# Recurrence stage of a bidirectional hybrid block: the inverse's products paired and moved, gate loads and chunk scalings re-placed

## The chip, the core and the metric

The kernel runs on one core of a Trainium2 chip. The metric is device time in microseconds (us) for one execution, the median of several. Five engines work side by side, each through its own queue in order: TensorE (PE in the profile; its weight loads are PEld), VectorE (DVE), ScalarE (ACT), GpSimd (POOL) and SyncE (SP), which here only issues DMAs. "The granted clock" (PEclk) is the share of TensorE's full speed that the chip allowed in a stretch.

## The reference

Cut to the part that the change touches; the other mixer, the projections and the MLP are left out.

```python
def _rwkv7_step(S, inp):
    """S_t = S_{t-1} diag(w_t) + (S_{t-1} a_t) b_t^T + v_t k_t^T ;  y_t = S_t r_t."""
    r, w, k, v, a, b = inp
    sa = jnp.einsum('bhvk,bhk->bhv', S, a)
    S = S * w[:, :, None, :] + sa[..., None] * b[:, :, None, :] + v[..., None] * k[:, :, None, :]
    y = jnp.einsum('bhvk,bhk->bhv', S, r)
    return S, y

# 8 heads of 64, 2048 tokens, once forward and once backward:
_, y_f = lax.scan(_rwkv7_step, S0, (r_s, ..., k_s, v_s, a_s, b_s))
_, y_b = lax.scan(_rwkv7_step, S0, (r_s, ..., k_s, v_s, a_s, b_s), reverse=True)
y = y_f + y_b                      # then a group norm per head, a bonus term, a gate g
...
merged = jax.nn.sigmoid(gate_a) * y_a + jax.nn.sigmoid(gate_b) * y_b
x = x + merged @ w_out
```

## The kernel before, in words

The kernel is one program of many stages. The change touches the recurrence stage. There the 2048 tokens are cut into 32 chunks of 64, and a loop runs over the steps s = 0 to 31; step s handles chunk s of the forward scan and chunk 31 - s of the backward one, for all 8 heads at once.

Within a step the recurrence is a chain: `st_W` (products of the chunk with the state X, evicted by ACT into W), `st_U` (W times the inverse TT, evicted by ACT into X), `st_S` (the state's increment; DVE adds it to gX and writes the next X, L1022; gX is then made by L999) and `st_Y` (the output, evicted by ACT). `sc_mm` computes the scores of a chunk LA = 7 steps ahead, for d = 0 and d = 1 apart; `sc_ev` evicts them: two DVE multiplies with a mask (Q, psc: L880, L881) and ACT copies (Nb, Lt: L887, L889). `tr_mm`/`tr_ev` transpose the operand bj of the next step, and `scale_bj` scales it by a decay: four ACT instructions for each d (L902).

The inverse TT is made for four chunks in both directions together, by the generator `invert`: DVE transposes the scores (XX, L919), runs 30 elimination steps (L924, L925), and transposes the result back in two halves into one buffer XC (L932). ACT copies each half into TT, four copies a half (L938); since XC is a single buffer, the second half waits for the first half's copies. DVE then makes the transposed result XT (L940), and TensorE forms the corner block in two products, first pz = Q times XT, then px = zs times TT, each for two halves hf = 0 and 1. The generator is cut by `yield`s: each plain `yield` gives up a VEC slot (`bg` takes one), each `yield "pe"` waits for a PE slot (`sl.tick(PE)`). It is started at the end of each fourth step and its TT is needed by the `st_U` of the fourth step after.

TensorE's free time is filled by `fill`, a generator of 312 slots of four 128x512 matmuls each: first 36 gate units (kind "g", six slots), then 32 output units (kind "y", three slots). The loop draws two slots at each of four places in a step (FW, F2, F3, F4), the part ahead of the loop draws others, and what is left follows the loop. Each change of weights brings a 512 KB load, an ACT cast (whi) and a DVE subtraction (wlo). A y unit loads its gate (`g_get`, into one of the three buffers `ev`), has ACT take the sigmoid in place (`g_sig`), and DVE multiplies it with the unit's PSUM result (L1221); the product goes out by DMA from the same buffer. In the last steps `gn_out` normalises the finished chunks, with some multiplies on POOL.

What sets the order: inside the loop PE, ACT, DVE and POOL work in the order in which the code is written (`manual_schedule`), each engine strictly one instruction after the other. The order of SP's loads is chosen by the framework's scheduler. Tags and `bufs` set which buffer a tile reuses, and so which instruction waits for which.

Of the kernel before, what the change touches and what calls it, by code (L numbers as in the profile page):

```python
# [166 lines left out]
def _body(tc, A, out, dump=None, upto=99):  # L167
# [749 lines left out]
    def invert(n):  # L917
# [22 lines left out]
        nc.vector.transpose(xt.rearrange("p b c -> p c b"), X)  # L940
        yield
        yield "pe"
        for hf in range(2):
            pz = cq.tile([128, 16, 32], F32, name="pz", tag="ptr")
            for u in range(16):
                sd, p = hf * 4 + u // 4, u % 4
                Q = qs[(n * 4 + sd // 2, sd % 2)][1]
                for e in range(2):
                    a0 = e * 64
                    nc.tensor.matmul(pz[a0 + 32:a0 + 64, u, :], Q[a0:a0 + 32, p, 32:64], xt[a0:a0 + 32, sd * 4 + p, :], start=True, stop=True)  # L950
            zs = cp.tile([128, 16, 32], F32, name="zs", tag="XX", bufs=2)
            nc.scalar.copy(out=zs[32:64], in_=pz[32:64])
            nc.scalar.copy(out=zs[96:128], in_=pz[96:128])
            yield "pe"
            px = cq.tile([128, 16, 32], F32, name="px", tag="ptr")
            for u in range(16):
                sd, p = hf * 4 + u // 4, u % 4
                for e in range(2):
                    a0 = e * 64
                    nc.tensor.matmul(px[a0:a0 + 32, u, :], zs[a0 + 32:a0 + 64, u, :], tt[a0 + 32:a0 + 64, sd, p, 32:64], start=True, stop=True)  # L960
            for e in range(2):
                a0 = e * 64
                (nc.scalar.copy if e else nc.vector.tensor_copy)(
                    out=tt[a0:a0 + 32, hf * 4:hf * 4 + 4, :, 32:64], in_=px[a0:a0 + 32].rearrange("r (a b) c -> r a b c", a=4))
            yield "pe"

# [67 lines left out]
    def gn_out(i):  # L1034
# [37 lines left out]
        for t in range(2):  # L1072
            nc.gpsimd.tensor_tensor(out=y8[t], in0=y8[t], in1=b8(rr[:, t * 8:t * 8 + 8]), op=ALU.mult)  # L1073
        yield
# [12 lines left out]
        for t, tt in enumerate(tiles):  # L1087
            nc.vector.tensor_tensor(out=o[t], in0=o[t], in1=bon[t], op=ALU.add)
            nc.gpsimd.tensor_tensor(out=o[t], in0=o[t], in1=gg[t], op=ALU.mult)
            sync.dma_start(out=d_ob[:, :, tt * 128:tt * 128 + 128], in_=o[t])  # L1090
# [31 lines left out]
    def fill():  # L1122
# [71 lines left out]
        for u, (kind, m, b) in enumerate(units):  # L1194
            if kind == "y":
                at(first[u] - 1, g_get, u)
                at(first[u] + 1, g_sig, u)

# [56 lines left out]
    bjs = [load_bj(1, d) for d in range(2)]  # L1255
    for d in range(2):
        scale_bj(1, d, bjs[d])
    for y in inv0:
# [12 lines left out]

    GN0, GNC, GNS = 27, [0], 3

# [5 lines left out]
    with tc.manual_schedule(engines=ORDERED):  # L1279
        for s in range(32):  # L1280
            la = s + LA
            last = s == 31
            st_W(s)
            bg(2)
            sl.tick(PE)
# [11 lines left out]
            if la < 32:  # L1297
                c = sc_mm(la, 0)
                sc_ev(c)
            bg(2)  # L1300
            sl.tick(PE)
# [3 lines left out]
            if not last:  # L1305
# [5 lines left out]
                st_g(s + 1)  # L1311
            st_Y(s)
            if la < 32:
                c = sc_mm(la, 1)
                sc_ev(c)
            if s % 4 == 0 and s < 28:
                sl.add(invert(s // 4 + 1))
            bg(2)
            sl.tick(PE)
            gn_tick(s, 1)  # L1320
            fil(F3)
            for d in range(2):
                if s < 30:
                    scale_bj(s + 2, d, bjs[d])
                bg(2)
                gn_tick(s, 2)
            sl.tick(PE)
            fil(F4)
    while gns or go.gens:
        gn_tick(32, 1)  # L1330
        fil()
    fil(1000)
# [486 lines left out]
```

## Time and profile before

| what | value |
|---|---|
| median of 3 runs | 3625.32 us (3624.73 to 3634.07) |
| profiled execution, its own time | 3635.12 us |
| its span in the profile | 3633.3 us |
| recurrence stage within the span, first slot of `fill` to the last transposes of `gn_out` | about 1052 to 1963 us |
| PE busy over the whole span | 3291.2 us (91%) |
| DVE / ACT / POOL busy | 2319.6 / 1569.8 / 1003.0 us |

The rows are read like this. A timeline row gives the start, the length, the engine, the line of the program, the operation and its operands, and in brackets how long the engine had been idle just before and whose end released it. A row of waits sums such idle times for one pair of instruction and releaser: total us, how often, the longest. Idle time matters on the engine that sets the pace; here that question has to be asked stretch by stretch.

### The profile page before, as it was taken

The numbers are of one execution on the slowest core, as the hardware profiler recorded it, in microseconds if no ns is written. First come the engines' busy times: TensorE is split into PE (matmuls) and PEld (weight loads), VectorE is DVE, ScalarE is ACT, GpSimd is POOL, SyncE is SP. The second block draws the span as 40 slices with busy tenths as digits, with TensorE's granted clock in tenths as the row PEclk, the third lists the DMA queues.
The fourth block names the chain that finished last, engine by engine and source line by source line (L and its number), as shares of the span: only waits on it lengthen the run. The fifth ranks groups of instructions, "written<-read, shape, count | busy, mean of one in ns | idle before, by whom it ended". The sixth has DMA issues, their size and how long they took to land. (4 is left out here: it accounts for less than half of the span.)

```text
span 3633.3 us, 58213 instructions
## 1 busy us (share of the span) xinstructions
PE 3291.2 (91%) x22232; PEld 2622.3 (72%) x22232; DVE 2319.6 (64%) x3913; ACT 1569.8 (43%) x2870; POOL 1003.0 (28%) x789
## 2 busy tenths in 40 slices
PE   7999999998978878877767899999989999999999
PEld 6787778766657666666655788877768777778887
DVE  5207764688846665666766466989899989724222
ACT  4214443555546666666544333434344443511111
POOL 1122222244430000000024412676766666100000
PEclk9999999999988999998988999999989999999999
DMA  4233444688883545555788746322232222523222
GB/s 148 91 118 109 134 137 134 197 224 229 230 247 108 158 151 158 153 182 177 216 244 271 286 140 199 115 76 79 78 125 96 81 76 82 168 86 115 83 83 64
DMA packets 403223, 531.30 MB, mean 146 GB/s; under 512 B 61504, under 2 KB 250560, under 8 KB 402944
## 3 DMA queue, kind: packets, MB, share of 16 engines
q1 hardware_dynamic: 402944, 527.58, 46.5%
q8 instruction: 175, 2.87, 0.3%
q14 instruction: 104, 0.85, 0.1%
HBM read 345.02 MB, written 181.93 MB: 145 GB/s over the span
## 5 line engine op out<-in xcount | busy, mean ns | idle before, releaser
L1553 POOL TENSOR_TENSOR rw<-rw 128x512 f32<-128x512 f32 x168 | 274.4, 1653 | 4.6 <-DVE cv L1598 1.2
L1706 PE MATMUL pd<-wdh,whi 128*128 128x512 f32 x672 | 261.6, 391 | 1.6 <-DVE ug L1498 1.6
L1707 PE MATMUL pd<-wdl,whi 128*128 128x512 f32 x672 | 261.4, 389 | 0.0
L1708 PE MATMUL pd<-wdh,wlo 128*128 128x512 f32 x672 | 259.3, 389 | 0.0
L241 PE MATMUL pg<-hhi,whi 128*128 128x512 f32 x928 | 249.0, 403 | 3.1 <-ACT whi L226 3.1
L241 PE MATMUL pg<-hlo,whi 128*128 128x512 f32 x928 | 250.5, 402 | 0.0
L241 PE MATMUL pg<-hhi,wlo 128*128 128x512 f32 x928 | 248.7, 403 | 0.0
L1073 POOL TENSOR_TENSOR Lt<-Lt,rnr 128x512 f32<-128x512 f32 x16 | 19.4, 1234 | 824.9 <-DVE rnr L254 766.5
L241 PEld LDWEIGHTS pg<-hhi,whi 128*128 128x128 f32 x928 | 176.2, 192 | 54.4 <-issue 14.3
L241 PEld LDWEIGHTS pg<-hhi,wlo 128*128 128x128 f32 x928 | 176.1, 192 | 49.8 <-issue 13.6
L241 PEld LDWEIGHTS pg<-hlo,whi 128*128 128x128 f32 x928 | 174.0, 191 | 52.4 <-issue 17.5
L227 POOL TENSOR_TENSOR wlo<-wraw,whi 128x1024 fp32r<-128x1024 f32 x46 | 114.9, 2498 | 349.6 <-PE pg L241 157.8
L1213 PE MATMUL pf<-fop,whi 128*128 128x512 f32 x576 | 172.6, 438 | 39.1 <-ACT whi L226 23.6
L1597 ACT ACTIVATE cv<-ug,vec 128x511 f32<-128x511 f32 (+1 forms) x88 | 71.9, 817 | 249.5 <-DVE ug L1498 249.5
L226 ACT CAST whi<-wraw 128x1024 fp32r<-128x1024 f32 x114 | 119.3, 1046 | 114.3 <-PE pg L241 50.8
L1213 PEld LDWEIGHTS pf<-fop,whi 128*128 128x128 f32 x576 | 113.7, 207 | 71.6 <-ACT whi L226 28.5
L1695 ACT CAST whi<-wraw 128x1024 fp32r<-128x1024 f32 (+1 forms) x36 | 35.2, 979 | 265.9 <-PE pd L1707 180.5
L1706 PEld LDWEIGHTS pd<-wdh,whi 128*128 128x128 f32 x672 | 126.1, 188 | 30.7 <-issue 5.0
L1598 DVE SCALAR_TENSOR_TENSOR cv<-ug,vec,cv 128x511 f32<-128x511 f32 (+1 forms) x88 | 125.0, 1421 | 35.8 <-ACT cv L1597 35.8
L227 DVE TENSOR_TENSOR wlo<-wraw,whi 128x1024 fp32r<-128x1024 f32 x68 | 83.7, 1231 | 99.4 <-ACT whi L226 98.8
L1708 PEld LDWEIGHTS pd<-wdh,wlo 128*128 128x128 f32 x672 | 126.2, 188 | 26.2
L1707 PEld LDWEIGHTS pd<-wdl,whi 128*128 128x128 f32 x672 | 126.2, 188 | 25.6
(470 smaller groups left out, 8274.4 us busy)
## 6 DMA issues: line engine op xcount, KB each, us to landing
rw<-wup SPq DMA_DIRECT2D x84, 512.0 KB, 3.5
wraw<-win SPq DMA_DIRECT2D x74, 512.0 KB, 4.1
Lt<-d_lt SPq DMA_DIRECT2D x64, 512.0 KB, 5.6
d_lt<-arbk SPq DMA_DIRECT2D x96, 256.0 KB, 3.9
d_gate<-ev SPq DMA_DIRECT2D x64, 256.0 KB, 3.5
X<-d_vt SPq DMA_DIRECT2D x64, 256.0 KB, 4.6
bj<-d_lt SPq DMA_DIRECT2D x128, 128.0 KB, 3.9
d_m<-ev SPq DMA_DIRECT2D x64, 256.0 KB, 5.4
```

The source lines that it names most:

```text
L226: (hi_eng or nc.scalar.copy)(out=hi, in_=src)
L227: (lo_eng or nc.vector).tensor_tensor(out=lo, in0=src, in1=hi.bitcast(F32), op=ALU.subtract)
L241: nc.tensor.matmul(ps, (wh, wh, wl)[ph], (xh, xl, xh)[ph], start=(ph == 0 and i == 0), stop=(ph == 2 and i == n - 1))
L1073: nc.gpsimd.tensor_tensor(out=y8[t], in0=y8[t], in1=b8(rr[:, t * 8:t * 8 + 8]), op=ALU.mult)
L1213: nc.tensor.matmul(ps, (wh, wh, wl)[ph][:, k0 + k, :], (hi, lo, hi)[ph][:, k, :], start=i == first[u] and k == 0, stop=i == last[u] and k ...
L1553: ps_ = lambda o, x, y, op: nc.gpsimd.tensor_tensor(out=o, in0=x, in1=y, op=op)
L1597: nc.scalar.activation(out=c, in_=u[:, c0:c0 + n], func=AF.Identity, scale=vc("cw1", m), bias=vc("cb", m))
L1598: nc.vector.scalar_tensor_tensor(out=c, in0=u[:, c0 - 1:c0 - 1 + n], scalar=vc("cw0", m), in1=c, op0=ALU.mult, op1=ALU.add)
L1695: nc.scalar.copy(out=ah[:, 0:n], in_=raw[:, 0:n])
L1706: nc.tensor.matmul(ps, a, wdh[k][:, cs], start=(k == 0), stop=False)
L1707: nc.tensor.matmul(ps, a, wdl[k][:, cs], start=False, stop=False)
L1708: nc.tensor.matmul(ps, l, wdh[k][:, cs], start=False, stop=False)
```

## The change

- `invert`: three more empty VEC slots between XT and the first product; pz of both halves in one PE slot, px of both halves in one PE slot, with a PE slot left empty between them. Half 1 takes its PSUM from the tag `psc` instead of `ptr`. The copies of px: both of half 0 on DVE, both of half 1 on ACT.
- The VEC slots of a step (`bg`): 14 before; now 12, and 14 in the fresh steps that start an inversion, of which 7 lie behind the start where 6 did.
- `g_get` is written two slots earlier, at the unit's first slot minus 3; `g_sig` one slot later, at its last slot.
- `scale_bj`: both directions were scaled behind F3; now d = 1 is scaled behind the W eviction and d = 0 behind the Y eviction.
- `gn_out`: both POOL multiplies go to DVE; the first `gn_out` starts at step 26 instead of 27; the loop behind the steps draws two fill slots a round instead of one.

```diff
@@ invert
         nc.vector.transpose(xt.rearrange("p b c -> p c b"), X)
         yield
+        for _ in range(3):
+            yield
         yield "pe"
+        zz = []
         for hf in range(2):
-            pz = cq.tile([128, 16, 32], F32, name="pz", tag="ptr")
+            pz = (cf.tile if hf else cq.tile)([128, 16, 32], F32, name="pz", tag="psc" if hf else "ptr", bufs=3 if hf else 1)
...
             nc.scalar.copy(out=zs[96:128], in_=pz[96:128])
-            yield "pe"
-            px = cq.tile([128, 16, 32], F32, name="px", tag="ptr")
+            zz.append(zs)
+        yield "pe"
+        yield "pe"
+        for hf in range(2):
+            px = (cf.tile if hf else cq.tile)([128, 16, 32], F32, name="px", tag="psc" if hf else "ptr", bufs=3 if hf else 1)
...
-                (nc.scalar.copy if e else nc.vector.tensor_copy)(
+                (nc.scalar.copy if hf else nc.vector.tensor_copy)(
                     out=tt[a0:a0 + 32, hf * 4:hf * 4 + 4, :, 32:64], in_=px[a0:a0 + 32].rearrange("r (a b) c -> r a b c", a=4))
-            yield "pe"
@@ gn_out
-            nc.gpsimd.tensor_tensor(out=y8[t], in0=y8[t], in1=b8(rr[:, t * 8:t * 8 + 8]), op=ALU.mult)
+            nc.vector.tensor_tensor(out=y8[t], in0=y8[t], in1=b8(rr[:, t * 8:t * 8 + 8]), op=ALU.mult)
...
-            nc.gpsimd.tensor_tensor(out=o[t], in0=o[t], in1=gg[t], op=ALU.mult)
+            nc.vector.tensor_tensor(out=o[t], in0=o[t], in1=gg[t], op=ALU.mult)
@@ fill
-                at(first[u] - 1, g_get, u)
-                at(first[u] + 1, g_sig, u)
+                at(first[u] - 3, g_get, u)
+                at(last[u], g_sig, u)
@@ ahead of the loop
-    for d in range(2):
-        scale_bj(1, d, bjs[d])
+    scale_bj(1, 0, bjs[0])
@@ the loop over the steps
-    GN0, GNC, GNS = 27, [0], 3
+    GN0, GNC, GNS = 26, [0], 3
...
             st_W(s)
+            if not last:
+                scale_bj(s + 1, 1, bjs[1])
             bg(2)
...
-            bg(2)
+            bg(1)
             sl.tick(PE)
             gn_tick(s, 1)
             fil(F2)
...
             st_Y(s)
+            if s < 30:
+                scale_bj(s + 2, 0, bjs[0])
...
-            bg(2)
+            bg(3 if fresh else 2)
             sl.tick(PE)
             gn_tick(s, 1)
             fil(F3)
-            for d in range(2):
-                if s < 30:
-                    scale_bj(s + 2, d, bjs[d])
-                bg(2)
-                gn_tick(s, 2)
+            bg(2)
+            gn_tick(s, 2)
+            bg(2 if fresh else 1)
+            gn_tick(s, 2)
             sl.tick(PE)
             fil(F4)
     while gns or go.gens:
         gn_tick(32, 1)
-        fil()
+        fil(2)
```

Three places show what this does to the order; all are the second inversion that the loop makes (started behind step 4, needed by step 8). On PE before, from the last scores of step 6 to the state products of step 7 (psc are scores, pf fill slots, pw and py the products of `st_W`):

```order
L874 MATMUL psc<-Lt 64x128 x16
L1213 MATMUL pf<-hhi_110,wlo 128x512 x4
L1213 MATMUL pf<-fop,whi 128x512 x4
L950 MATMUL pz<-XT,Q 32x32 x32
L1213 MATMUL pf<-fop,whi 128x512 x4
L1213 MATMUL pf<-fop,wlo 128x512 x4
L985 MATMUL pw<-X,Lt 64x64 x16
L992 MATMUL py<-X,Lt 64x64 x16
L960 MATMUL px<-TT_8672,zs 32x32 x32
```

On PE now, from the same scores on (ptr is the transpose of bj, pu the products of `st_U`):

```order
L874 MATMUL psc<-Lt 64x128 x16
L1218 MATMUL pf<-fop,whi 128x512 x8
L1218 MATMUL pf<-fop,wlo 128x512 x4
L1218 MATMUL pf<-fop,whi 128x512 x4
L990 MATMUL pw<-X,Lt 64x64 x16
L997 MATMUL py<-X,Lt 64x64 x16
L1218 MATMUL pf<-fop,whi 128x512 x4
L1218 MATMUL pf<-fop,wlo 128x512 x4
L908 MATMUL ptr<-ident,bj 128x128 x4
L1014 MATMUL pu<-W,TT_8673 64x64 x16
L874 MATMUL psc<-Lt 64x128 x16
L953 MATMUL pz<-XT,Q 32x32 x64
```

The first product stood between F3 and F4 of step 6; now it stands behind the first scores of step 7, with both halves together.

On DVE before, the end of the same inversion around the state update of step 6 (X, gX):

```order
L924 TENSOR_TENSOR tm<-XX 128x30
L925 TENSOR_TENSOR XX<-XX,tm 128x30
L928 MEMSET XX 128x32
L932 STREAM_TRANSPOSE XC<-XX 128x16x32
L1022 TENSOR_TENSOR X<-pS,gX 64x8x64 x2
L999 TENSOR_TENSOR gX<-X,gall 64x512 x2
L880 TENSOR_TENSOR Q<-psc,mk_8666 128x512
L881 TENSOR_TENSOR psc<-psc,mk_8666 128x512
L932 STREAM_TRANSPOSE XC<-XX 128x16x32
L940 STREAM_TRANSPOSE XT<-XX 128x32x32
```

On DVE now:

```order
L1027 TENSOR_TENSOR X<-pS,gX 64x8x64 x2
L1004 TENSOR_TENSOR gX<-X,gall 64x512 x2
L880 TENSOR_TENSOR Q<-psc,mk_8670 128x512
L881 TENSOR_TENSOR psc<-psc,mk_8670 128x512
L924 TENSOR_TENSOR tm<-XX 128x58
L925 TENSOR_TENSOR XX<-XX,tm 128x2x29
L924 TENSOR_TENSOR tm<-XX 128x30
L925 TENSOR_TENSOR XX<-XX,tm 128x30
L928 MEMSET XX 128x32
L932 STREAM_TRANSPOSE XC<-XX 128x16x32
L227 TENSOR_TENSOR fop<-ev,fop 128x512 x2
L932 STREAM_TRANSPOSE XC<-XX 128x16x32
```

The last two elimination steps and the first half of XC stood ahead of the state update and now stand behind it; XT follows directly, as before.

On ACT before, from the evictions of step 6's last scores to the W of step 7:

```order
L889 COPY Lt<-psc 64x512 x2
L938 COPY TT_8672<-XC 32x32x16 x4
L1217 COPY ev<-pf 128x512
L902 ACTIVATE bj<-bj,gall 128x128 x4
L938 COPY TT_8672<-XC 32x32x16 x4
L902 ACTIVATE bj<-bj,gall 128x128 x4
L952 COPY zs<-pz 32x512
L953 COPY zs<-pz 32x512
L226 CAST whi<-wraw 128x1024
L226 CAST fop<-ev 128x512 x2
L987 COPY W<-pw 128x512
```

On ACT now, from the same evictions on:

```order
L889 COPY Lt<-psc 64x512 x2
L226 CAST fop<-ev 128x512 x2
L938 COPY TT_8672<-XC 32x32x16 x6
L992 COPY W<-pw 128x512
L902 ACTIVATE bj<-bj,gall 128x128 x4
L938 COPY TT_8672<-XC 32x32x16 x2
L1222 COPY ev<-pf 128x512
L913 COPY bkt<-ptr 128x512
```

The scalings no longer stand ahead of W, and two of the four copies of the second half of XC now follow it; six copies, two of them from the second half, stand ahead of it.

## Rows read from the trace of the kernel before

**Rows 1.** Busy time by stretch: from:to, length, busy by engine, PEclk, DMA, GB/s.

```profile
1172.30:1734.00 561.70, 444.41 (x7900) 365.99 (x7896) 344.57 (x658) 368.08 (x803) 0.00 (x0) 0.91 0.53 164
1734.00:1908.00 174.00, 120.39 (x1605) 97.51 (x1600) 117.99 (x232) 87.56 (x182) 21.62 (x16) 0.85 0.78 232
1908.00:1963.00 55.00, 32.33 (x110) 24.14 (x109) 42.10 (x96) 26.96 (x59) 23.12 (x16) 0.72 0.79 253
```

**Rows 2.** PE's waits from 1040 to 1945 us: total us, times, longest.

```profile
PE pz L950 <- DVE XT L940: 73.1, 8, 14.2
PE pf L1213 <- ACT whi L226: 45.9, 18, 11.2
PE pu L1009 <- ACT W L987: 16.8, 10, 6.1
```

**Rows 3.** PE timeline, steps 4 to 7: start, us, instruction, [idle before, releaser].

```profile
1247.24 1.15 PE L985 MATMUL pw<-X,Lt 128*64 128x64 f32 x32
...
1251.74 1.09 PE L1009 MATMUL pu<-W,TT 64*64 64x64 f32 x30
...
1259.21 0.96 PE L1213 MATMUL pf<-hlo,whi 128*128 128x512 f32 x3
...
1263.06 1.15 PE L985 MATMUL pw<-X,Lt 128*64 128x64 f32 x32
...
1277.99 1.20 PE L1213 MATMUL pf<-hhi,whi 128*128 128x512 f32 x4 [2.04 <-ACT whi L226]
...
1314.14 1.92 PE L950 MATMUL pz<-XT,Q 32*32 32x32 f32 x64 [14.18 <-DVE XT L940]
1315.98 2.08 PE L1213 MATMUL pf<-fop,whi 128*128 128x512 f32 x4
...
1321.32 1.20 PE L960 MATMUL px<-TT,zs 32*32 32x32 f32 x64
```

**Rows 4.** DVE timeline: first, second and seventh inversion of the loop.

```profile
1172.31 2.17 DVE L919 STREAM_TRANSPOSE XX<-Nb 128x1024 f32<-128x1024 f32 x1 [0.68 <-ACT Nb L887]
...
1262.21 2.15 DVE L919 STREAM_TRANSPOSE XX<-Nb 128x1024 f32<-128x1024 f32 x1 [0.68 <-ACT Nb L887]
...
1300.67 0.21 DVE L924 TENSOR_TENSOR tm<-XX 128x58 f32<-128x58 f32 x1
...
1302.64 1.36 DVE L1022 TENSOR_TENSOR X<-pS,gX 64x512 f32<-64x512 f32 x2
...
1311.12 1.09 DVE L932 STREAM_TRANSPOSE XC<-XX 128x512 f32<-128x512 f32 x1 [4.37 <-ACT TT L938]
...
1733.94 2.07 DVE L919 STREAM_TRANSPOSE XX<-Nb 128x1024 f32<-128x1024 f32 x1 [0.68 <-ACT Nb L887]
```

**Rows 5.** ACT timeline, the end of the second inversion.

```profile
1306.18 1.22 ACT L887 COPY Nb<-Q 32x128 f32<-32x128 f32 x4 [5.76 <-DVE Q L880]
1307.41 1.17 ACT L889 COPY Lt<-psc 64x512 f32<-64x512 f32 x2
1308.60 2.49 ACT L938 COPY TT<-XC 32x512 f32<-32x512 f32 x4
...
1320.51 0.59 ACT L987 COPY W<-pw 128x512 f32<-128x512 f32 x1 [0.54 <-PE pw L985]
```

**Rows 6.** PE timeline at the start of the loop, step 0.

```profile
1147.48 1.92 PE L960 MATMUL px<-TT,zs 32*32 32x32 f32 x64 [3.85 <-ACT zs L953]
...
1158.38 1.86 PE L1009 MATMUL pu<-W,TT 64*64 64x64 f32 x29
```

**Rows 7.** Waits of ACT and of SP's queue for the gates, 1040 to 1945 us.

```profile
ACT ev L1192 <- DMA ev<-d_gate: 51.3, 13, 9.9
...
SPq L1189 <- DMA d_m<-ev: 70.8, 24, 8.2
```

**Rows 8.** The end of the stage: a PE timeline row, and POOL's multiply by line.

```profile
1917.45 2.11 PE L1081 MATMUL psc<-ident,Lt 128*128 128x128 f32 x8 [9.11 <-POOL Lt L1073]
...
L1073 POOL TENSOR_TENSOR Lt<-Lt,rnr 128x512 f32<-128x512 f32 x12 | 14.0, 1186 | 824.9 <-DVE rnr L254 766.5 <-DMA Lt<-d_y 27.9 <-DMA Lt<-d_bon 16.0
```

More of the change, by code (lines that the diff above doesn't have):

```diff
@@ L959, in invert @@
                     a0 = e * 64
-                    nc.tensor.matmul(px[a0:a0 + 32, u, :], zs[a0 + 32:a0 + 64, u, :], tt[a0 + 32:a0 + 64, sd, p, 32:64], start=True, stop=True)
+                    nc.tensor.matmul(px[a0:a0 + 32, u, :], zz[hf][a0 + 32:a0 + 64, u, :], tt[a0 + 32:a0 + 64, sd, p, 32:64], start=True, stop=True)
             for e in range(2):
                 a0 = e * 64
-                (nc.scalar.copy if e else nc.vector.tensor_copy)(
+                (nc.scalar.copy if hf else nc.vector.tensor_copy)(
                     out=tt[a0:a0 + 32, hf * 4:hf * 4 + 4, :, 32:64], in_=px[a0:a0 + 32].rearrange("r (a b) c -> r a b c", a=4))
-            yield "pe"
     def load_x(s):
@@ L1282, in _body @@
             last = s == 31
+            fresh = s % 4 == 0 and s < 28
             st_W(s)
+            if not last:
+                scale_bj(s + 1, 1, bjs[1])
             bg(2)
@@ L1315, in _body @@
                 sc_ev(c)
-            if s % 4 == 0 and s < 28:
+            if fresh:
                 sl.add(invert(s // 4 + 1))
-            bg(2)
+            bg(3 if fresh else 2)
             sl.tick(PE)
```

## The prediction, made before the changed kernel ran

> **What bounds the kernel now.** I read the busy times by stretch first. The diff touches only the recurrence stage, so the stretches around it keep their times. Within the stage no engine is full: from the first inversion of the loop to the seventh, 561.7 us, PE is busy for 444.4, ACT for 368.1 and DVE for 344.6 us, and the granted clock averages 0.91 [rows 1]. Such shares hide what limits each part, so I went to PE's waits. The largest is the first product pz, waiting for DVE's transpose XT: 73.1 us in 8 waits, one for each inversion; behind it come fill slots that wait for ACT's cast whi, 45.9 us in 18, and `st_U` waiting for W, 16.8 us in 10 [rows 2].
>
> The PE timeline says how much there is to win. An undisturbed step runs from 1247.24 to 1263.06, 15.8 us [rows 3]. A period of four steps with four products of some 1.2 us would so need 4 x 15.8 + 4.8 = 68.1 us. The six periods between the first and the seventh inversion of the loop take (1733.94 - 1172.31) / 6 = 93.6 us each [rows 4]: 25.5 us of each are waiting and slow clock.
>
> In the second inversion DVE starts at 1262.21, when PE has just passed the second scores of step 4, and writes the state X of step 6 at 1302.64 + 1.36 = 1304.00, 41.8 us later [rows 4]. The order of DVE puts every state update behind the elimination steps written ahead of it. PE stands idle for 14.18 us until 1314.14, waiting for XT [rows 3]. So the path of this part runs through DVE and, at its end, to and fro between DVE and ACT: ACT idles 5.76 us for Q, copies Nb and Lt, then the first half of XC into TT for 2.49 us, and DVE waits 4.37 us for those copies before the second half [rows 4, 5].
>
> **The change part by part.** The new place of the products does not shorten DVE's work by one instruction. It puts more of PE's work ahead of the wait: F4 of step 6 (1.9 us), and of step 7 all up to the first scores. I add up a period of the second inversion along what ends last.
>
> (a) From the start of the inversion to X of step 6: 41.8 us before. The last two elimination steps and the first half of XC, from 1300.67 to 1302.64, 2.0 us, now stand behind this update [rows 4]: 39.8 us.
>
> (b) From X to W of step 7. W is now behind six TT copies on ACT, and two of these need the second half of XC. From X at 1304.00 to the end of Q at 1306.18 2.2 us; Nb and Lt 2.4; four copies 2.5; the half of XC 1.1; two copies half of 2.5, 1.25; the W copy 0.6 [rows 4, 5]: 10.05, and 0.75 for an ACT instruction of a fill slot that stands between: 10.8 us. XT on DVE is done by then, so pz itself waits no more; the wait moves to the state products and to `st_U`.
>
> (c) From `st_U` of step 7 to the next inversion: a step without its first 4.5 us (1247.24 to 1251.74), 11.3 us; four products, 4.8; from step 8's start to the inversion as from 1247.24 to 1262.21, 15.0 [rows 3, 4]: 31.1. After the long wait pz took 1.92 against 1.20 and a fill slot 2.08 against 1.20 us [rows 3], which fits the lower level of the clock, 1.2 against 2.4 GHz. I estimate 2.2 us for this a period, before and after, since a wait of some 6 us for W remains; and 1.0 us for the transposition that waits for the buffer `ptr` behind the zs copies, now four in a row. 34.3 us.
>
> Together 39.8 + 10.8 + 34.3 = 84.9. The same sum on the kernel before, 41.8 + 10.1 to pz + 1.9 + 15.8 + 4.8 + 15.0 + 2.2 + 1.1 = 92.7, falls 0.9 short of 93.6, small waits for whi; added, 85.8. That is 7.8 us an inversion, and I take 8, for seven inversions **56 us**. Bounds: 4 an inversion if X is no earlier and the copies around W cost 2 us more; 13 if the divided wait leaves the clock up, `ptr` is free and DVE waits 2 us less for ACT (the scalings, no longer ahead of whi and W, let ACT reach whi earlier; a wait of 2.04 us left the clock up [rows 3]). So 28 to 91.
>
> The order of ACT is what keeps (b) long. ACT stood idle 5.76 us at Nb with copies written behind it [rows 5]; it passes nothing. The Trainium skill ("TensorE: Matmul & The Clock Gate", the architectural detail on queue depths) calls the queues of ScalarE and VectorE strictly first in, first out. If ACT could take W ahead of the copies, `st_U` would start some 6 us sooner, and pz would be held only by XT, about 2 us a period less: seven times that would make the sum 14 us better; by the rule and the row it is not.
>
> **The first products, ahead of step 0.** There px waited 3.85 us for zs, and the halves followed one another, product and copies in turn, until `st_U` at 1158.38, 10.9 us behind the first px [rows 6]. With both halves at once one round of copies goes. The order also puts four more fill slots (4.1 us) there, which now cover the copies and are missing at the end of the stage. I take **5 us**, between 2 (copies on ACT as late as before) and 8.
>
> **The gates.** Written earlier is not loaded earlier. A gate lands in one of three buffers `ev`, which the previous output of two units before, or a load of the fill's operand, leaves only when its DMA has landed: SP already waits for d_m 24 times, 70.8 us [rows 7], 2.95 us each. Moving the load up two slots leaves that bound where it is. What is real is the sigmoid, one slot later: a slot is 15.8 / 8 = 2.0 us, and ACT's 13 waits for gates, 51.3 us, 9.9 the longest [rows 7], shrink by up to 2.0 each, at most 26 us. About half of it holds W or a transposition that PE needs. **10 us**, between 0 and 25.
>
> **The rest.** The transposes of `gn_out` cost PE one wait of 9.11 us for POOL; POOL's multiply took 1.19 us [rows 8], where DVE's adds took 0.68 each [rows 4]. 32 of them are some 22 us of DVE in the last 170 us of the stage, in which DVE has 69 us idle (174.0 - 118.0 and 55.0 - 42.1) [rows 1]: covered, but each stands ahead of a fill product in DVE's order. One step's head start for `gn_out` takes seven of its slots out of the last 55 us, of which PE is busy 32 [rows 1]. The four slots moved to the front cost this end nothing while it waits. **6 us**, between -4 (multiplies in DVE's way) and 15.
>
> Sum: 56 + 5 + 10 + 6 = 77 us. The profiled execution took 3635.1 us outside, 3633.3 in its span, 10 over the median of 3625.3; I take the gain off both: 3558 for such an execution, **3548** for the median. With all lower bounds (28 + 2 + 0 - 4 = 26) 3599, with all upper ones (91 + 8 + 25 + 15 = 139) 3486.
>
> **The rivals.**
> - The stall only moves. If X of step 6 is as late as before, and W follows it by 9 us more than in (b), the 8.9 us of PE work set ahead of pz are eaten. For: DVE does the same work, and ACT's chain through XC now stands in front of W. Against: the longest part of (b) was in the path before too. It leaves the start and a little of the gates: 3617.
> - DVE stops being the bound. If the scalings behind the evictions let ACT keep up, and DVE with it, a period nears PE's own 68.1 + 4 = 72 us: 21 x 7 + 21 = 168 off, 3457. Against: (a) is mostly DVE's own work, and none of it is taken away.
> - The gates do come early, as the words of the change say: then ACT's 51.3 us go, and of PE's losses some 35 instead of 10: 3523. Against: the ring of three buffers.
> - Slower: the gate's early load blocks SP. It is now issued behind d_m at once and holds the loads of bj, X and weights behind it until d_m has landed. Before, 24 holds of 2.95 us. If each doubled and PE saw all of it, 24 x 5.9 = 142 us would be lost, 3690; from 77 / 24 = 3.2 us a unit on the change is slower than before. Against: SP's order is chosen apart from the engines', and already puts most loads behind such a wait.
>
> The Trainium skill ("DMA: Bandwidth & Descriptors", Anatomy of one DMA) says that DMA engines don't wait on semaphores, the issuing sequencer does, before it dispatches. That speaks against writing a load ahead of its free buffer, and for the last rival; SP's 70.8 us [rows 7] agree that the wait is SP's.
>
> **How the numbers follow.** A change of 0.3%, 11 us, is about what a measurement of this kernel can tell from none. Forecast 0.65; early gates 0.13; DVE no bound 0.08; the stall only moves 0.07, which counts as the same; slower 0.07. Faster so has 0.86. The range takes the forecast with its bounds and the early gates, 0.78, and a little of the faster side: 3490 to 3600.
>
> **What would show it.** Right: periods between inversions of 84 to 87 us; pz with hardly a wait; new waits of `st_W` for X and of `st_U` for W, some 6 to 9 us together an inversion, the latter behind ACT's TT copies; SP's waits at the gate about as long as before. Wrong: periods below 80, then DVE's lag was not the path; pz still waiting 5 us or more, then XT is later than (b) says; `st_S` or the transposition waiting for X or bj loads in steps 21 to 31, then the gates block SP.

## The result, and the profile after

| kernel | median | ratio to before, 95% interval |
|---|---|---|
| before | 3627.57 us (4 runs) | 1 |
| after | 3572.49 us (3569.51 to 3574.50, 4 runs) | 0.9845 [0.9828, 0.9862] |

The changed kernel is 1.55% faster, some 56 us. The forecast was 77 us and 3548; the time lies inside the range of 3490 to 3600. Below, the gain of a kernel is always (1 - ratio) x 3630 us, 3630 being about the median of before over all comparisons; intervals of 0.0009 to 0.0019 to either side mean that such a gain is known to 3 to 7 us, and the difference of two of them mostly to 8 or 9.

The profiled span fell from 3633.3 to 3568.9 us. That is 9 us more than the medians are apart, since the profiled execution of before was a long one (3635.12 us against a median of 3627.57); a stretch read from one execution of each carries such differences. By stretch, from after's own inversions: busy times and clock (from:to, length, busy by engine, PEclk, DMA, GB/s), to set beside [rows 1]:

```profile
1166.88:1690.91 524.03, 440.37 (x7873) 363.48 (x7872) 345.42 (x660) 369.35 (x803) 0.00 (x0) 0.93 0.58 177
1690.91:1842.60 151.69, 109.18 (x1494) 88.74 (x1494) 115.72 (x240) 81.44 (x170) 0.00 (x0) 0.85 0.87 249
1842.60:1997.40 154.80, 124.97 (x614) 98.46 (x613) 96.67 (x168) 69.66 (x117) 55.44 (x37) 0.90 0.90 313
```

The first line is the stretch from the first to the seventh inversion of the loop, 561.7 us before [rows 1]. PE's idle time in it fell from 117.3 us (561.7 - 444.4) to 83.7, its busy time only by 4.0: the gain is waiting taken away. The second line is the seventh inversion to the start of step 31 (161.0 before), the third from there to the first product with `w_out` (164.4 before); the merge of the two mixers, whose products begin some 51 us behind the start of step 31 in both kernels, lies within it.

The inversions themselves, DVE timeline of after (start, us, instruction, [idle before, releaser]): the first, second, third, sixth and seventh, and the second state update within the second one.

```profile
1166.88 2.05 DVE L919 STREAM_TRANSPOSE XX<-Nb 128x1024 f32<-128x1024 f32 x1 [0.68 <-ACT Nb L887]
...
1250.93 2.07 DVE L919 STREAM_TRANSPOSE XX<-Nb 128x1024 f32<-128x1024 f32 x1 [0.68 <-ACT Nb L887]
...
1290.03 1.38 DVE L1027 TENSOR_TENSOR X<-pS,gX 64x512 f32<-64x512 f32 x2
...
1336.23 2.18 DVE L919 STREAM_TRANSPOSE XX<-Nb 128x1024 f32<-128x1024 f32 x1 [0.68 <-ACT Nb L887]
...
1593.55 2.19 DVE L919 STREAM_TRANSPOSE XX<-Nb 128x1024 f32<-128x1024 f32 x1 [0.68 <-ACT Nb L887]
...
1690.91 2.01 DVE L919 STREAM_TRANSPOSE XX<-Nb 128x1024 f32<-128x1024 f32 x1 [0.68 <-ACT Nb L887]
```

The five periods between the first and the sixth take (1593.55 - 1166.88) / 5 = 85.3 us, where before they took 92.4. The sixth, 97.4 us, is hardly shorter than before, where it was 99.6.

PE's waits over these six periods, before and after (total us, times, longest; [rows 2] have the whole stage). Before, 1172.30 to 1734.00:

```profile
PE pz L950 <- DVE XT L940: 65.4, 6, 14.2
PE pf L1213 <- ACT whi L226: 21.8, 11, 4.7
PE pu L1009 <- ACT W L987: 7.8, 7, 1.5
PE ptr L908 <- ACT zs L953: 7.6, 6, 1.3
```

After, 1166.88 to 1690.91:

```profile
PE pf L1218 <- ACT whi L226: 45.8, 11, 8.4
PE pf L1218 <- ACT fop L226: 12.2, 2, 6.2
PE pu L1014 <- ACT W L992: 8.8, 4, 4.9
```

The wait of pz for XT, 65.4 us, is gone, and most of the 7.6 us behind zs (2.0 now). Half of it came back elsewhere: fill products now wait 58.0 us for operands that ACT casts, whi and fop, where they waited 21.8. The balance of these rows is close to the 33.6 us of idle time above.

Where such a wait comes from is seen on ACT and PE in the second inversion. ACT of after:

```profile
1293.59 1.22 ACT L887 COPY Nb<-Q 32x128 f32<-32x128 f32 x4 [3.57 <-DVE Q L880]
...
1296.04 1.14 ACT L226 CAST fop<-ev 128x512 fp32r<-128x512 f32 x2
1297.09 2.50 ACT L938 COPY TT<-XC 32x512 f32<-32x512 f32 x4
...
1302.02 0.59 ACT L992 COPY W<-pw 128x512 f32<-128x512 f32 x1
```

PE of after, beside it:

```profile
1296.71 1.31 PE L1218 MATMUL pf<-fop,whi 128*128 128x512 f32 x2 [6.15 <-ACT fop L226]
...
1303.66 1.09 PE L1014 MATMUL pu<-W,TT 64*64 64x64 f32 x30
```

DVE makes Q only behind the late state update, ACT's Nb waits for Q, and the cast of fop stands behind Nb in ACT's order and waits for nothing of its own (it has no idle time before it). So here DVE's lag reaches PE by way of a cast, at a fill slot, and not by way of W or XT.

The waits for the gates, from 1040 to 1945 us, to set beside [rows 7]; the last line is before's, of the same stretch:

```profile
ACT ev L1197 <- DMA ev<-d_gate: 25.8, 7, 6.5
...
DVE ev L1226 <- ACT ev L1197: 41.2, 13, 5.9
...
SPq L1194 <- DMA d_m<-ev: 51.1, 21, 4.9
```

```profile
DVE ev L1221 <- ACT ev L1192: 19.5, 10, 4.1
```

ACT lost 25.5 us of its waits for gates, about the prediction's upper bound (26). DVE's product now waits 21.7 us more for the sigmoid. It looks as if the wait had been handed on, but these rows can't tell what the gates' new place did from what the rest of the change did; `e5_gates_only` and `e1_gates_back` below can.

### The profile page after: what moved, and what is told of

Its sections match the earlier page's. It is cut to its first block, busy times and chain, and to the rows that moved or that the text cites. A ratio compares the mean times of both kernels' runs of the same rounds, so it can differ in the third digit from the quotient of the medians.

```text
span 3568.9 us, 58167 instructions
## 1 busy us (share of the span) xinstructions
PE 3280.0 (92%) x22232; PEld 2612.0 (73%) x22232; DVE 2328.1 (65%) x3945; ACT 1571.5 (44%) x2870; POOL 957.1 (27%) x757
## 4 chain that ended last, share of the span: by engine, by line
PE 32%; DVE 22%; issue 6%; DMA 6%; ACT 5%; POOL 1%; SPq 1%; DVEq 0%; ACTq 0%; POOLq 0%
PE pg L241 7%; PE pu L1501 6%; PE pd L1714 4%; PE pd L1715 4%; PE pd L1716 4%; DVE cv L1606 3%; PE pf L1218 2%; DVE ug L1506 2%; DVE s1l L227 2%; DVE uv L1506 2%; DVE tm L924 1%; DVE XX L925 1%; DMA d_m<-ev 1%; POOL s3l L227 1%; DVE cv L1607 1%
## 5 line engine op out<-in xcount | busy, mean ns | idle before, releaser
L1613 ACT ACTIVATE cv<-cv 128x511 f32<-128x511 f32 (+1 forms) x84 | 52.9, 630 | 198.4 <-DVE cv L1607 198.4
L1706 DVE TENSOR_TENSOR wlo<-wraw,whi 128x1024 fp32r<-128x1024 f32 (+1 forms) x36 | 39.3, 1092 | 150.5 <-ACT whi L1703 150.5
```

## The experiments

The theory after this reading, A: the place of the inverse's products carries the gain; the gates and the output norm carry none; what stalls now is DVE's lag, felt at casts on ACT. Its rivals: the gates come early and help; the scalings carry the gain; the norm's move does.

### One part alone on the kernel before, and the inverse with the scalings

`e3_inverse_only` has the edits of `invert` and the slots of `bg`. The pairing, the later place, the second PSUM tag and the split of the copies go together in it, so it can't say which of them counts. Cut to three of its places:

```diff
-            yield "pe"
-            px = cq.tile([128, 16, 32], F32, name="px", tag="ptr")
+            zz.append(zs)
+        yield "pe"
+        yield "pe"
+        for hf in range(2):
...
-            bg(2)
+            bg(3 if fresh else 2)
```

> The kernel before with the products of the inverse paired and moved, and the slots of a step that go with them; gates, scalings and the output norm stay as before. Theory A (the placement of the inverse carries the gain): before minus 40 to 50 us, the wait of the first product pz for XT falls from 73.1 us to under 10, periods between inversions 84 to 88 us. Rival B (the placement only pays together with the scalings, which before stand ahead of whi and W on ACT): less than 25 us, periods still above 90, and the waits for W and whi on PE larger than the 18.3 and 83.8 us of the changed kernel.

Measured: 0.9884 [0.9866, 0.9903], 42 us. The six periods take 532.9 us instead of 561.6, and pz waits 2.6 us in all. As A expects, but for the periods: 85.6 to 89.5 in the first five, where it had 84 to 88. Of rival B's sign, longer waits for W and whi, nothing is seen (11.0 and 81.3 us).

`e4_scale_only`, the scalings:

```diff
-    for d in range(2):
-        scale_bj(1, d, bjs[d])
+    scale_bj(1, 0, bjs[0])
...
+            if not last:
+                scale_bj(s + 1, 1, bjs[1])
...
+            if s < 30:
+                scale_bj(s + 2, 0, bjs[0])
```

> The kernel before with only the chunk scalings placed behind the evictions of W and Y. Theory A: within 6 us of before, since pz goes on waiting for XT about 73 us. Rival B (the scalings carry the gain): 20 us or more faster, with the 92.2 us in which DVE waits for whi cut by half and the wait of pz below 50 us.

Measured: 0.9980 [0.9971, 0.9989], 7 us, and pz still waits 76.7 us. The scalings alone carry little, 6.7 us in the six periods (561.6 to 554.9).

`e5_gates_only`:

```diff
-                at(first[u] - 1, g_get, u)
-                at(first[u] + 1, g_sig, u)
+                at(first[u] - 3, g_get, u)
+                at(last[u], g_sig, u)
```

> The kernel before with only the gates re-placed: load written two slots earlier, sigmoid one slot later. The prediction gave this 10 us (0 to 25). Theory A after reading the changed kernel's trace (the wait for the gate's DMA only moves from ACT's sigmoid to DVE's multiply, since a ring of three buffers still bounds the load): within 5 us of before, ACT's waits for gates fall from 51.3 to about 26 us and DVE's multiply waits for the sigmoid about 20 us more than its 19.5 us. Rival B (the gate comes earlier): 10 to 25 us faster, both waits smaller together than the 70.8 us of before.

Measured: 1.0009 [1.0000, 1.0018], 3 us slower, at the edge of what the interval tells from none. Its waits from 1040 to 1945 us:

```profile
ACT ev L1192 <- DMA ev<-d_gate: 37.8, 8, 7.7
...
DVE ev L1221 <- ACT ev L1192: 39.7, 15, 6.0
...
SPq L1189 <- DMA d_m<-ev: 68.4, 24, 7.3
```

51.3 + 19.5 = 70.8 us before [rows 7] are now 37.8 + 39.7 = 77.5: ACT waits 13.5 us less and DVE 20.2 more. SP's queue waits for d_m just as often and as long as before, 24 times, 68.4 against 70.8 us. From the issue of a gate's load by SP to the start of its sigmoid on ACT 9.5 us pass on the average of the 32 gates, where it was 8.5 before, though the edit puts the two three slots, some 6 us, further apart. So a load written earlier is hardly issued earlier, and the rival of early gates falls. The Trainium skill ("DMA: Bandwidth & Descriptors", Anatomy of one DMA) says that the issuing sequencer waits and not the DMA engine; the 24 waits, which are SP's, agree with it.

Two of PE's waits on the kernel before, and the same two with a third of `e5_gates_only`, from 1040 to 1945 us:

```profile
PE ptr L908 <- ACT bkt L913: 11.7, 4, 6.0
PE ptr L908 <- ACT bj L902: 8.2, 4, 5.6
```

```profile
PE pz L950 <- DVE XT L940: 81.6, 8, 14.2
...
PE ptr L908 <- ACT bkt L913: 5.2, 2, 2.8
...
PE ptr L908 <- ACT bj L902: 2.6, 3, 0.9
```

The later sigmoid does spare the transposition, 12.1 us of waiting, as the prediction had it. But pz waits 8.5 us more for XT (73.1 before [rows 2]), which DVE makes, and no time is gained.

`e13_inverse_and_scale` has the edits of the first two together.

> The kernel before with the inverse's placement and the scalings behind the evictions, gates and output norm as before. The prediction's terms for this are 56 + 5 = 61 us. Apart, the two gave 41 and 6 us. Theory A (they add up): 44 to 50 us faster than before. Rival B (they help one another, since the scalings no longer stand ahead of the W that the paired products wait for): 52 to 61 us.

Measured: 0.9843 [0.9830, 0.9857], 57 us, the whole gain of the change without gates and norm. The two parts give 42 and 7 apart and 57 together, a number in rival B's range. Yet the difference of 8 us is known to some 9 only, and the traces don't bear B out: in the six periods the scalings save 6.7 us on the kernel before and 7.9 on top of the inverse (532.9 to 525.0), and the spans of the profiled executions fall by 50.0 and 10.2 us apart and by 55.0 together. That the parts help one another is not shown. ACT in the second inversion of `e3_inverse_only` shows where the scalings stand in the way:

```profile
1301.93 1.27 ACT L902 ACTIVATE bj<-bj,gall 128x128 f32<-128x128 f32 x4
1303.11 2.48 ACT L938 COPY TT<-XC 32x512 f32<-32x512 f32 x4
1305.61 1.28 ACT L902 ACTIVATE bj<-bj,gall 128x128 f32<-128x128 f32 x4
...
1308.09 0.59 ACT L992 COPY W<-pw 128x512 f32<-128x512 f32 x1
```

Eight scalings, 2.55 us, stand ahead of W, four of them ahead of the first TT copies too. With the scalings behind the evictions DVE waits less for the copies of XC: over the six periods 13.3 us in `e13_inverse_and_scale` against 19.6 in `e3_inverse_only`, six waits each.

### One part taken back from the changed kernel

`e2_sigmoid_back` writes the sigmoid one slot earlier again, and leaves the early load:

```diff
-                at(last[u], g_sig, u)
+                at(first[u] + 1, g_sig, u)
```

> The changed kernel with the sigmoid back at its former slot, one earlier; the load stays early. Theory A (the later sigmoid makes DVE wait 41.2 us for it, and DVE's wait delays the state in steps 21 to 31): 3 to 10 us faster than the changed kernel, DVE's wait for the sigmoid falls to 20 us or less, and the sixth period falls from 97.4 to about 94. Rival B (the later sigmoid is what spares ACT): 5 to 15 us slower, with ACT's waits for gates back near 50 us and PE's waits for W and bkt up.

Measured: 0.9853 [0.9836, 0.9869], 53 us against 56: no difference that these intervals show. Theory A's gain of 3 to 10 us did not come, and the rival's loss of 5 to 15 is not shown. DVE's wait for the sigmoid fell from 41.2 to 28.9 us, where A had 20 or less, and the sixth period stayed at 97.9. The transposition of bj waited 15.7 us in two waits for bkt, ACT's copy, which both times stood behind a sigmoid that ACT had waited to start: the wait went to yet another place.

`e1_gates_back` puts load and sigmoid back:

```diff
-                at(first[u] - 3, g_get, u)
-                at(last[u], g_sig, u)
+                at(first[u] - 1, g_get, u)
+                at(first[u] + 1, g_sig, u)
```

> The changed kernel with load and sigmoid of the gates back at their former slots. Alone on the kernel before, the re-placement cost 4 us; the sigmoid alone put back in the changed kernel cost about 3. Theory A (the ring of three buffers bounds the load, the wait only changes its engine): within 5 us of the changed kernel, ACT's waits for gates back at 35 to 50 us and DVE's for the sigmoid down from 41.2 to about 20. Rival B (in the changed kernel, whose steps are shorter, the early load counts): 8 us or more slower.

Measured: 0.9864 [0.9847, 0.9881], 49 us, 7 under the changed kernel, between A's 5 and B's 8; the intervals overlap. Its waits from 1040 to 1945 us, of ACT, DVE and PE:

```profile
ACT ev L1197 <- DMA ev<-d_gate: 21.8, 7, 7.1
```

```profile
DVE ev L1226 <- ACT ev L1197: 21.3, 6, 6.7
```

```profile
PE ptr L908 <- ACT bkt L913: 13.9, 2, 7.7
```

A had ACT's waits back at 35 to 50 us and was wrong: they are 21.8 with the gates at their former slots, and 25.8 in the changed kernel. So it is not the gates' new place that keeps ACT's waits low in the changed kernel; `e3_inverse_only`, without any other part, already has 25.0. What the new place does in the changed kernel is to add 19.9 us to DVE's wait for the sigmoid and 8.3 us to the fill's wait for DVE's products (6.5 to 14.8), and to take away the 13.9 us for bkt.

`e9_gn_back` puts the norm back as it was: both multiplies on POOL, the start at step 27, one fill slot a round behind the loop. Cut to two places:

```diff
-            nc.vector.tensor_tensor(out=o[t], in0=o[t], in1=gg[t], op=ALU.mult)
+            nc.gpsimd.tensor_tensor(out=o[t], in0=o[t], in1=gg[t], op=ALU.mult)
...
-    GN0, GNC, GNS = 26, [0], 3
+    GN0, GNC, GNS = 27, [0], 3
```

> The changed kernel with the output norm as before: both multiplies on POOL, the first norm at step 27, one fill slot a round behind the loop. The prediction had 6 us (-4 to 15) for this part. The parts timed alone so far add up to 41 (inverse) + 6 (scalings) - 4 (gates) = 43 us, the whole change gives 56; 12 to 13 us are not accounted for. Theory A: the norm's move is worth them, so this run is 8 to 14 us slower than the changed kernel, all of it behind the seventh inversion. Rival B: the parts help one another inside the loop (scalings behind the evictions pay more once the inverse is paired); then this run is within 4 us of the changed kernel and its periods are the same 84 to 87 us.

Measured: 0.9843 [0.9827, 0.9859], 57 us: the norm's move is worth nothing that can be seen within some 8 us, and its periods are the changed kernel's. Theory A, 8 to 14 us for the norm, falls. The time is as rival B of this run had it, but what the 10 us are by which the parts apart (42 + 7 - 3) fall short of the whole stays open: the errors of the four runs together come to as much. With these the four cases of gates and norm, on top of inverse and scalings, are:

| | norm as before | norm moved |
|---|---|---|
| gates as before | 57.0 us (`e13_inverse_and_scale`) | 49.4 (`e1_gates_back`) |
| gates moved | 57.0 (`e9_gn_back`) | 56.3 (the change) |

Neither part gains over the first field. Whether the norm on DVE costs 7 us where the sigmoid stands early, as the one odd field says, these runs don't settle. `e2_sigmoid_back`, with 53 us, is such a case too and points the same way.

### What the gates cost

`e14_after_no_gate` leaves out load and sigmoid; DVE copies where it multiplied. `e15_before_no_gate` has the same edit on the kernel before.

```diff
-                at(first[u] - 3, g_get, u)
-                at(last[u], g_sig, u)
+                pass
...
-                    gt = gts.pop(u)
-                    nc.vector.tensor_tensor(out=gt, in0=ps, in1=gt, op=ALU.mult)
+                    gt = ev.tile([128, 512], F32, name="ev", tag="ev")
+                    nc.vector.tensor_copy(out=gt, in_=ps)
```

> The changed kernel with the gates of the output units left out: no load, no sigmoid, and DVE copies the unit's PSUM result where it multiplied, so that the merged output lacks its gate. It stands beside the same edit on the kernel before. Theory A (the waits for gates, now DVE's, 41.2 us, eat what the inverse's placement should give from step 21 on): the sixth period falls from 97.4 to 90 or less, and this run gains 15 to 30 us on the changed kernel, at least 8 more than the same edit gains on the kernel before. Rival B (the gain is less there because DVE has more work in a step, casts and subtractions for weights and operands, and ACT's cast whi comes late for it): the sixth period stays above 94, the gain is under 12 us and about the same on both kernels.

> The kernel before with the gates left out in the same way: no load, no sigmoid, a DVE copy in place of the product, so that the merged output lacks its gate. ACT's waits of 51.3 us for gates go. Theory A (gates cost the changed kernel more than this one): 5 to 12 us faster than before, the sixth period near 97. Rival B (they cost both the same): as much as the edit gains on the changed kernel, within 5 us.

Measured: `e14_after_no_gate` 0.9759 [0.9745, 0.9772], 31 us beyond the changed kernel; `e15_before_no_gate` 0.9950 [0.9936, 0.9963], 18 us. Both are more than A's 15 to 30 and 5 to 12. The difference, 13 us, is more than A's 8, though the intervals together leave it uncertain by some 9. The edit takes away load, sigmoid and the wait for a buffer at once, so it can't say which of them costs. The sixth and seventh inversions on DVE's timeline, of `e14_after_no_gate` and then of `e15_before_no_gate`:

```profile
1593.72 2.18 DVE L919 STREAM_TRANSPOSE XX<-Nb 128x1024 f32<-128x1024 f32 x1 [0.68 <-ACT Nb L887]
...
1684.62 2.06 DVE L919 STREAM_TRANSPOSE XX<-Nb 128x1024 f32<-128x1024 f32 x1 [0.68 <-ACT Nb L887]
```

```profile
1636.82 2.19 DVE L919 STREAM_TRANSPOSE XX<-Nb 128x1024 f32<-128x1024 f32 x1 [0.68 <-ACT Nb L887]
...
1734.40 2.05 DVE L919 STREAM_TRANSPOSE XX<-Nb 128x1024 f32<-128x1024 f32 x1 [0.68 <-ACT Nb L887]
```

Without gates the sixth period falls from 97.4 to 90.9 in the changed kernel and from 99.6 to 97.6 in the old one. So in that period the gates take 4.5 us more from the changed kernel than from the old one, and they explain that much of the 5.8 us by which its gain (2.2) stays under 8. From the seventh inversion to step 31 they cost both about the same (13.0 and 15.0 us). The rest of the shortfall there is not theirs.

### Where the remaining stall sits

If PE now waits at fill slots for casts that stand late in ACT's order, their place should decide. `e8_weights_early` writes cast and subtraction of a new weight two slots earlier:

```diff
-        puts = [max(first[u] - 2, done_[wid[fresh[i - 2]]] + 1 if i > 1 else 0) for i, u in enumerate(fresh)]
+        puts = [max(first[u] - 4, done_[wid[fresh[i - 2]]] + 1 if i > 1 else 0) for i, u in enumerate(fresh)]
```

> The changed kernel with the cast whi and the subtraction wlo of each new weight tile written two slots earlier. PE's largest wait is now the fill product that waits for ACT's cast whi, 83.8 us in 19 waits, some 4.4 us each; a slot is about 2 us. Theory A (the cast is late because it stands behind copies of ACT that wait for DVE, so its place decides): the wait falls to 45 us or less and 10 to 30 us are gained on the changed kernel. Rival B (the wait is DVE's lag, and any product of PE that comes next waits for it in its place): whi's wait falls, but st_W's wait for X and the scores' for Q take over, and the time stays within 5 us. Rival C (the weight's load is not there yet): ACT's wait for wraw rises above 40 us, and the time is the same or worse.

Measured: 0.9811 [0.9797, 0.9824], 69 us, 12 more than the changed kernel. Its waits on PE from 1040 to 1945 us:

```profile
PE pu L1014 <- ACT W L992: 28.4, 9, 10.5
PE pf L1218 <- DVE ev L1226: 27.0, 9, 7.3
PE pf L1218 <- ACT whi L226: 26.8, 6, 10.1
PE pf L1218 <- ACT fop L226: 18.6, 3, 7.1
```

The wait for whi falls from 83.8 to 26.8 us, as A expects. Of these 57 us only 12 reach the end, known to 8; W, the gates' products and fop take up 29 (they were 18.3, 14.8 and 12.2), and the scores' wait for Q, which rival B named, is 9.0. A and rival B both have a part: about a fifth of the wait came off the time, the rest only changed the instruction that waits. The periods show it too: the first and the fourth are 7.0 and 6.4 us shorter than the changed kernel's, the second 5.8 us longer.

`e7_w_first` moves one VEC slot, so that all four copies of the second half of XC stand behind W:

```diff
-            bg(2)
+            bg(2 if fresh else 3)
...
-            bg(2 if fresh else 1)
+            bg(1 if fresh else 0)
```

> The changed kernel with one VEC slot of a step moved in the steps that don't start an inversion, so that the four ACT copies of the second half of XC all stand behind W, where two stood ahead of it. Step (b) of the prediction had 10.8 us from X to W, of which 1.1 for that half of XC and 1.25 for its two copies. Theory A (W is on the path): W comes about 2 us sooner in each inversion, PE's wait for W falls from 18.3 to about 6 us, and 7 to 14 us are gained. Rival B (XT and the state update behind it are the path, not W): periods stay at 84 to 87 us, pz waits for XT again by what W gained, and the time stays within 4 us.

Measured: 0.9816 [0.9802, 0.9829], 67 us, 10 more than the changed kernel, again known to 8. The size is A's, the path is not: PE's wait for W fell only from 18.3 to 16.1 us. ACT of `e7_w_first` in the second inversion shows W behind the first four copies, where in the changed kernel six stood ahead of it and it began at 1302.02:

```profile
1296.23 2.50 ACT L938 COPY TT<-XC 32x512 f32<-32x512 f32 x4
1299.18 0.58 ACT L992 COPY W<-pw 128x512 f32<-128x512 f32 x1 [0.45 <-PE pw L990]
```

Set against the copies ahead of it, W comes some 2 us earlier, but PE did not wait for it here in either kernel. In the first inversion a cast of whi stands between the copies and W; there the two copies fewer show at the fill slot that needs whi. PE of after, and of `e7_w_first`:

```profile
1213.61 2.07 PE L1218 MATMUL pf<-hhi,whi 128*128 128x512 f32 x4 [5.71 <-ACT whi L226]
```

```profile
1212.53 2.08 PE L1218 MATMUL pf<-hhi,whi 128*128 128x512 f32 x4 [3.35 <-ACT whi L226]
```

2.4 us less of waiting, and the first period falls from 84.0 to 81.7. The next four change by 0.8 us or less each, the sixth falls from 97.4 to 94.0. So the edit works where a cast stands behind the copies, and in the output units; how in the latter was not followed.

`e12_w_first_weights_early` has both edits.

> The changed kernel with both: W ahead of all four copies of the second half of XC (alone 10.5 us faster than the changed kernel) and the new weights cast two slots earlier (alone 12 us faster). Theory A (they shorten different stretches: the first the 2 us at the end of each inversion, the second PE's waits for whi in all steps): 19 to 25 us faster than the changed kernel. Rival B (both only move the same wait of PE, which is set by DVE's lag in an inversion): 10 to 15 us faster, as one alone.

Measured: 3556.42 us, 0.9786 [0.9772, 0.9801], 78 us: 21 more than the changed kernel, nearly the sum of the two (12 and 10), as A expects. The intervals leave it 13 to 29, so the upper end of rival B, 15, is not quite excluded. PE's waits over its six periods (1169.99 to 1681.83, 511.8 us):

```profile
PE pf L1218 <- ACT whi L226: 12.8, 3, 4.5
PE pf L1218 <- ACT fop L226: 12.8, 2, 7.1
PE pz L953 <- ACT bkt L913: 10.2, 4, 2.8
```

This version is faster than both kernels. Over these periods no single wait is left that stands out.

## Why the prediction was right or wrong

**The path through an inversion, (a) to (c): right.** In the second inversion X of the second step ends at 1290.03 + 1.38 = 1291.41, 40.5 us behind the start at 1250.93; (a) said 39.8. W ends at 1302.61, 11.2 later; (b) said 10.8. `st_U` starts 1.05 later, and from there to the next inversion at 1336.23 are 32.6 us; (c) said 34.3 with no gap. The sum is 85.3, the forecast 85.8 with the small waits; the mean of the first five periods is 85.3. pz waits no more, as said. The clock was to cost the same before and after; its mean in the six periods rose from 0.91 [rows 1] to 0.93, and PE's busy time fell by 4.0 of 444.4 us, so its part in the gain is small.

**Where the wait would reappear: wrong.** The prediction put it on `st_W` for X and `st_U` for W, 6 to 9 us an inversion. W's wait stayed where it was (8.8 us in six periods against 7.8). It is the fill's casts that wait, since they too stand in ACT's order behind Nb. Step (b) listed ACT's instructions up to W, but not that one of them, fop or whi, is needed by the fill slot in front of `st_W`. Time and place differ here: the period came out right because both waits hang on the same ACT queue. In the rows shown here ACT takes nothing ahead of its order, as the prediction assumed. The Trainium skill ("TensorE: Matmul & The Clock Gate", architectural detail, queue depths) calls the queues of ScalarE and VectorE strictly first in, first out; the 6.15 us that PE waited for a cast behind Nb agree with it.

**The term of the inverse: seven times 8 was the wrong way to multiply.** The 93.6 us of before were a mean with a sixth period of 99.6 in it; the first five took 92.4, so the gain there is 7.1 us each and not 7.8. The sixth period gained 2.2. By `e13_inverse_and_scale`, whose parts the terms 56 + 5 stand for, the sum is 57 against 61. Yet its trace shows that this agreement has two errors in it that cancel, so the size of the sum is in part luck. From the sixth inversion to step 31 it gained 4.8 us (2.8 + 2.0), where 16 were forecast: there the output units run, whose gates, casts and products stand between DVE's elimination steps. Behind step 31 it gained 13.0, where the forecast had none. (In the changed kernel the two stretches beside step 31 gained 9.3 and 9.6; against `e9_gn_back`, 159.3 and 151.2 us, the norm's move shortens the first by 7.6 and lengthens the second by 3.6.)

**The first products: 5 forecast, 3 to 8 found.** From the inversion ahead of the loop to the first one of the loop 68.4 us became 60.4 here, and 60.6 to 65.0 in the variants with the paired products: 3 to 8 us, about the bounds, though 147 matmuls of the fill run there in the changed kernel where 126 did.

**The four slots at the front: "cost this end nothing" was wrong, in the good direction.** Behind step 31 the fill has 69 matmuls left instead of 85 (x45 + 24, x56 + 29), 16 for the four slots. Rows of that stretch (line, engine, operation, tiles, count, busy us, mean ns, idle before), of before and then of `e13_inverse_and_scale`:

```profile
L1213 PE MATMUL pf<-fop,whi 128*128 128x512 f32 x56 | 16.6, 442 | 5.7 <-ACT whi L226 5.7
...
L1081 PE MATMUL psc<-ident,Lt 128*128 128x128 f32 x32 | 8.0, 427 | 13.7 <-POOL Lt L1073 13.7
```

```profile
L1218 PE MATMUL pf<-fop,whi 128*128 128x512 f32 x45 | 13.4, 439 | 3.8 <-DVE ev L1226 3.8
...
L1086 PE MATMUL psc<-ident,Lt 128*128 128x128 f32 x32 | 5.7, 306 | 3.8 <-POOL Lt L1078 3.7
```

With the products of fop and wlo, 29 in 9.1 us and 24 in 7.4, 4.9 us of products and 11.9 us of waits are less there, with POOL's multiplies unchanged; 9.5 us come back as waits of the merge's products for ACT's cast bh (6.5 before, 16.0 now). That the earlier end of the fill is what shortens POOL's wait was not tried apart.

**The gates: 10 forecast, none shown.** The ring of three buffers was seen rightly, and the rival of early gates rightly set against it. The step that failed is the next one: ACT's waits shrink, so about half reaches PE. In `e5_gates_only` ACT's waits shrank by 13.5 us, and PE's waits for bkt, bj and W by 14.4 (6.5 + 5.6 + 2.3), as the prediction had it. But the sum had no term for DVE, whose multiply stands behind the sigmoid: it waited 20.2 us more, pz 8.5 us more for DVE's XT, and the time was 3 us longer instead of shorter. On top of inverse and scalings the new place is worth 0 us with the norm as before and 7 with the norm moved, both known to 8 or 9; so in the changed kernel the forecast 10 is not excluded, but nothing shows it.

**The rest: 6 forecast, nothing found.** `e9_gn_back` does without it at the same time, within some 8 us, which by itself leaves room for 6. PE's waits for POOL were sized by one of 9.11 us; up to 1945 us there were five, 21.7 us in all. With the multiplies on DVE, PE's transposes of the norm wait 11.8 us for DVE where those of `e9_gn_back` wait 17.0 for POOL: most of this wait, too, went to DVE.

So 16 of the 21 us by which the sum was too large are these last two terms. Together they gave -1 us (56.3 against the 57.0 of `e13_inverse_and_scale`), known to 8. That the time lay inside the range all the same is due to the range, which had gates and rest down to 0 and -4, while the forecast of 77 counted on 16.

Of the rivals, "the stall only moves" has half a truth: 36 of the 65 us that pz gave up came back as waits for casts. "DVE stops being the bound" fell: the periods are 85 us and not 72. The slower rival fell: SP's waits at the gate are 51.1 us and not 142; that they would stay as long as before, 70.8, was wrong too.

## What to carry over

Where every engine keeps its order, a product that is moved out of a wait only helps as far as the next instruction that hangs on the same late engine; look for it among the casts and copies of unrelated work, not only along the chain that was moved. Taking a wait off one engine gained nothing here where the next engine in the chain took it over: ask who waits behind it. Writing a load earlier gained nothing either, while it waited for a buffer whose last output had not landed. And before parts of one edit are said to help one another, set the difference (57 us together, 42 + 7 apart) against the errors of all the runs in it, and look into the traces.
